# Pairs of w_in cut into scaled fp16 parts instead of fp32r parts

## The chip, the cores and the metric

One Trainium2 chip, one core of it. The metric is the device time of one execution in microseconds (us). The core has a matrix engine (TensorE, PE in the profile, with its weight loads as PEld), a vector engine (VectorE, DVE), a scalar engine (ScalarE, ACT), a general engine (GpSimd, POOL), and SyncE (SP), which here issues the transfers. Each engine works through its own queue in order and waits for the others by semaphores.

## The reference

One layer of a diffusion backbone, for 128 context tokens and 512 latent tokens (640 columns in all), width 1024. All inputs are fp32.

```
u = rms_norm(h, g_pre1) * (1 + sc1) + sh1
z = u @ w_in                      # 1024 x 6656: q, k, v, b_gate, c_gate, x_in, g_att, g_conv
q, k normalised per head, axial rotary on latent tokens
att  = block_attention(q, k, v) @ w_att_out
conv = (b_gate * dwconv3(c_gate * x_in)) @ w_conv_out
merged = sigmoid(g_att) * att + sigmoid(g_conv) * conv
h = h + g1 * rms_norm(merged @ w_o, g_post1)
u = rms_norm(h, g_pre2) * (1 + sc2) + sh2
h = h + g2 * rms_norm((silu(g) * val) @ w_down, g_post2)   # g, val = dwconv3(u @ w_up)
```

The shifts, scales and gates (sh1, sc1, g1, ...) come from a small product of two conditioning vectors with w_ada. The change concerns `u @ w_in` for the columns of g_att (all but the first 256), c_gate, x_in, b_gate and g_conv.

## The kernel before

**Precision.** A product of two fp32 matrices is made of three matmuls: each operand x is cut into hi, x rounded to fp32r (ScalarE, a copy), and lo = x - hi (VectorE), and hi*hi + hi*lo + lo*hi is summed in PSUM. The pools `whi` and `wlo` hold three such cuts of 128 x 1024 each.

**Stages.** Attention first; then eight products with w_att_out (`plain_gemm`, j = 0 to 7), in which the right operands of the next stage are made (`making`); then the stage of the 19 pairs; then eight products with w_conv_out, then w_o, and the feed-forward part, about half of the span.

**The pairs.** A pair is 256 columns of w_in (two raw tiles a1 and a2 of 128 x 1024, the reduction's eight blocks side by side). `PAIRS` lists them: GA 1 to 3, then four times C, X, B, then GC 0 to 3; pair 0 is the first. `mix` computes a pair with 640 tokens as a 2 x 2 block product by Strassen's method in Winograd's form: seven products instead of eight, each with 12 matmuls of 320 columns (four blocks of the reduction, three matmuls each). The seven, in the order of TensorE, are A11, A12, S2, S1, S3, S4, A22. Their left operands are four "parts" of weights: part 0 is a1 itself (A11, A12), part 1 holds two sums of the pair's blocks (S1, S2), part 2 two further sums (S3, S4), part 3 half of a2 (A22). The sums are made by VectorE (`msums`, three steps adds[0], adds[1], adds[2]), the cuts by `mhi` (ScalarE) and `lo_of` (VectorE). The right operands are the blocks B11, B21, B22 of u and four combinations T1 to T4 of them, all cut once for the stage; in the trace B blocks are read from UH and UL, the T from MT.

Between products ScalarE copies partial results out of PSUM (`copied`: p1 after A11, u2 after S2, p5 after S1; `mix_last` after A22) and VectorE adds them (`added`). S3 accumulates into the bank that u2 is copied from.

**Order.** In this part the queues of PE, ACT and DVE are the order of the code: `mix(m)` also issues the first cuts and sums of pair m + 1, and `extra` holds what follows from pair m - 1, by slots 0 to 6 between the products: after GA and GC two sigmoids, after GA two multiplications, after X the multiplications, two copies and taps of the convolution (L1564, L1565, L1500), after B the last tap, the multiplications and the cut of the finished rows (BHa, BHb by L1506, BL). SP's queue is put in order by a scheduler.

**Loads.** `mload` loads one raw tile (512 KB) into a pool of three, two per pair. `SHIFTS` says in which pair and slot a step of the second shift vector is made (`shift_add`: two instructions of 768 columns on VectorE, L342, then the load of the next row block into the one buffer XG). `shift_rows` and `shift_columns` fold the result with matmuls and transfers.

Of the kernel before, what the change touches and what calls it, by code (L numbers as in the profile page):

```python
# [112 lines left out]
def trunk_layer(ctx, tc, x_prompt, x_sample, cache_k, cache_v, c, c_ctx, w_ada, b_ada, g_pre1, g_post1, g_pre2,  # L113
# [1192 lines left out]
    for i in range(2):  # L1306
        for h in range(2):
            TT[f"mB{i + 1}{h + 1}"] = tuple(x[:, 4 * i:4 * i + 4, h * HT:(h + 1) * HT] for x in (UH, UL))
    TAG = {"T1": "r5a", "T2": "r5b", "T3": "r6a", "T4": "r6b"}
# [6 lines left out]
    def whole(out, name):  # L1316
        hi, lo = TT["m" + name]
# [8 lines left out]
    making = [  # L1326
        lambda: whole(Xa, "B11"), lambda: whole(Xb, "B12"), lambda: minus(Xa, Xa, Xb), lambda: whole(Xc, "B22"),
        lambda: right_of("T1", Xa), lambda: minus(Xb, Xc, Xb), lambda: minus_both(Xc, Xa, Xc), lambda: right_of("T3", Xb),
        lambda: whole(Xd, "B21"), lambda: right_of("T2", Xc), lambda: minus_both(Xd, Xc, Xd), lambda: right_of("T4", Xd)]
# [25 lines left out]
    def mload(n):  # L1355

        if n < 2 * NP:
            x, i = PAIRS[n // 2]
            col_load(("m", n // 2, n % 2), w_in, AT[x] + (2 * i + n % 2) * 128)
        elif n < 2 * NP + KT:  # L1360
            col_load(("v", n - 2 * NP), w_conv_out, (n - 2 * NP) * 128)
# [21 lines left out]
    def mix(m, extra):  # L1383
# [3 lines left out]
        pair["m", m] = tuple(bank((3 * m + i) % 8)[:, 0:HT] for i in range(3))  # L1387
# [12 lines left out]
        lo_of(("m", m, 1))  # L1400
# [9 lines left out]
        lo_of(("m", m, 2))  # L1410
# [6 lines left out]

        copied(("m", m), "p5", 2, HT)
# [6 lines left out]

        added(d1[:, HT:], ("m", m), "p5", 0)
        lo_of(("m", m, 3))
        mload(2 * m + 4)
        if nxt:
            mhi(nxt, 0)  # L1430
            lo_of(("m", nxt, 0))
            adds[1]()
        else:
            vcut(0)
# [8 lines left out]
        mload(2 * m + 5)  # L1443
# [6 lines left out]
    def times(out, a, b, sign=1.0):  # L1450
        if sign == 1.0:
# [9 lines left out]
    for j in range(KT):  # L1461
        unit = next_unit()
        if j == 6:
            for n in range(3):
                mload(n)
        if j < 6:
            for f in making[2 * j:2 * j + 2]:
                f()
        elif j == 7:
            adds = msums(0)  # L1470
            adds[0]()
            mhi(0, 0)
            lo_of(("m", 0, 0))
# [3 lines left out]
            mload(3)  # L1477
# [24 lines left out]
    def sigma(x, sign=1.0):  # L1502
        S.activation(x, x, AF.Sigmoid, scale=sign)
# [8 lines left out]
    XG = region(ra, "r2b", [5 * 512], F32, "XG")  # L1512
    xaccs, xraw = [[XG[:, i * 768:i * 768 + 768]] for i in range(2)], XG[:, 1536:2304]
    SHIFTS = {(0, 4): 0, (1, 1): 1, (2, 1): 2, (3, 1): 3, (4, 4): 4, (7, 4): 5, (10, 1): 6, (10, 4): 7}
# [26 lines left out]
    for m, (x, i) in enumerate(PAIRS):  # L1541
        ex = {}
        if m == 11:
            shr = shift_rows()
        elif m == 14:
            shift_columns(shr, bank(5))
# [6 lines left out]
        if before[0] in ("GA", "GC"):  # L1553
            r0, r1 = mrows(m - 1)
            also(1, sigma, r0)
            also(1, sigma, r1, -1.0)
# [12 lines left out]
        elif before[0] == "B":  # L1569
            c0, c1, y0, y1, b0, b1 = ROWS[:6]  # L1570
            also(0, conv_tap, y1, c1, o, 2)
            also(1, times, y0, b0, y0)
            also(1, b_hi, e, y0)
            also(1, times, y1, b1, y1, -1.0)
# [13 lines left out]
    sigma(ROWS[6])  # L1588
    sigma(ROWS[7], -1.0)
# [24 lines left out]
    for j in range(KT):  # L1614
# [4 lines left out]
        if 0 < j < KT - 3:  # L1619
            mload(2 * NP + j + 3)  # L1620
# [11 lines left out]
        outs = plain_gemm(j + 2, hi, lo, BH, BL)  # L1632
        sg = ROWS[j]
# [891 lines left out]
```

## Time and profile before

| | |
|---|---|
| median of 3 runs | 1074.8 us (1074.75 to 2641.38) |
| span of the profiled execution, first to last instruction | 1073.0 us |
| its mean granted TensorE clock | 0.999 |
| stage of the 19 pairs | 286.28 to 520.75 us of the span, 234.47 us |
| PE busy in that stage | 234.47 us |
| DVE busy in that stage | 196.91 us |
| ACT busy in that stage | 115.41 us |

The profiled execution is given with its span only; its own time lies above that by what comes ahead of the first and after the last instruction, which for the median is 1.8 us. One of the three runs, 2641.38 us, stands alone; the other two are 0.05 us apart.

In a row of the timeline the first number is the start in us from the span's start, the second the duration, then engine, line, instruction, output <- inputs, shapes (out <- in), count, and in brackets the idle time before it and what ended it. A row that stands for several instructions has the duration from the first start to the last end. Rows of groups give total busy time and the mean duration in ns; after the second bar the idle time of the engine ahead of them. TensorE's matmuls overlap, so the time of one in a stream is read from start to start.

### The profile page before, as it was taken

The page shows a single profiled execution, that of the slowest core. Times are in us where ns is not written, and L with a number is a line of the kernel's source. Part 1 is how long each engine was busy: PE and PEld are TensorE (multiplying, and loading weights), DVE is VectorE, ACT ScalarE, POOL GpSimd, SP SyncE. Part 2 cuts the span into 40 slices and gives each one's busy share as a digit, 9 for nine tenths or more (in the row PEclk, how much of TensorE's full clock was granted, in tenths as well). Part 3 has the DMA queues.
Part 4 walks back from the last instruction along what each step waited for, and adds up shares of the span by engine and source line. Part 5 has one row for each costly group of instructions (what it writes and reads, how often), then busy time and mean ns, then how long its engine had stood idle before and what let it go on. Part 6 is the DMA issues. An engine that isn't in the chain of part 4 may idle for free.

```text
span 1073.0 us, 20652 instructions
## 1 busy us (share of the span) xinstructions
PE 1056.8 (98%) x8216; PEld 995.4 (93%) x8216; DVE 899.9 (84%) x1379; ACT 598.4 (56%) x1057; POOL 133.1 (12%) x162
## 2 busy tenths in 40 slices
PE   8999999999999999999999999999999999999997
PEld 6788898899999999999998789999999999999996
DVE  5699999865498999896599678889999988989897
ACT  5478999942344544445322366645555555546673
POOL 1087676500000000000000020000000000000001
PEclk9999999999999999999999999999999999999999
DMA  9829999962244333223668634434544534436873
GB/s 320 256 82 175 190 168 187 191 147 60 75 123 124 93 103 94 79 79 99 189 188 253 198 131 129 121 116 136 166 131 152 150 122 131 152 116 219 277 275 115
DMA packets 243197, 164.02 MB, mean 153 GB/s; under 512 B 94874, under 2 KB 216214, under 8 KB 243102
## 3 DMA queue, kind: packets, MB, share of 16 engines
q1 hardware_dynamic: 242990, 162.68, 55.5%
q8 instruction: 64, 1.05, 0.4%
q14 instruction: 31, 0.25, 0.1%
q10 hardware_dynamic: 112, 0.04, 0.0%
HBM read 123.31 MB, written 17.36 MB: 131 GB/s over the span
## 4 chain that ended last, share of the span: by engine, by line
PE 90%; DVE 3%; ACT 2%; DMA 1%; POOL 1%; issue 1%; SPq 1%; DVEq 0%; ACTq 0%; POOLq 0%
PE b L1274 47%; PE b L235 10%; PE b L237 10%; PE b L236 9%; PE s L709 4%; PE s L1073 2%; PE s L1170 2%; PE s L235 1%; PE s L237 1%; PE s L1162 1%; PE s L478 1%; DVE marks L1120 1%; PE s L236 1%; PE b L1900 1%; ACT P L1134 1%
## 5 line engine op out<-in xcount | busy, mean ns | idle before, releaser
L1274 PE MATMUL b<-ZBr,whi 128*128 128x320 f32 x688 | 152.1, 309 | 0.0
L1274 PE MATMUL b<-MT,whi 128*128 128x320 f32 x608 | 134.4, 309 | 0.0
L1274 PEld LDWEIGHTS b<-ZBr,whi 128*128 128x128 f32 x688 | 114.9, 188 | 0.1
L1274 PE MATMUL b<-ZBr,wlo 128*128 128x320 f32 x344 | 106.1, 308 | 0.0
L1274 PEld LDWEIGHTS b<-MT,whi 128*128 128x128 f32 x608 | 101.7, 188 | 0.0
L1274 PE MATMUL b<-MT,wlo 128*128 128x320 f32 x304 | 94.0, 309 | 0.0
L1261 ACT ACTIVATE whi<-SUM 128x1024 fp32r<-128x1024 f32 x40 | 42.2, 1055 | 78.3 <-DVE SUM L1813 75.7
L1843 DVE SCALAR_TENSOR_TENSOR Y<-C,cffn,Y 128x642 f32<-128x642 f32 x88 | 77.9, 886 | 0.9
L1261 ACT ACTIVATE whi<-WB 128x1024 fp32r<-128x1024 f32 x38 | 40.2, 1058 | 55.5 <-DVE WB L1368 55.5
L1274 PE MATMUL b<-ZBT,whi 128*128 128x320 f32 x320 | 71.0, 308 | 0.0
L1274 PE MATMUL b<-UL,whi 128*128 128x320 f32 x228 | 70.8, 311 | 0.0
L1274 PE MATMUL b<-UH,wlo 128*128 128x320 f32 x228 | 70.1, 307 | 0.0
L1274 PE MATMUL b<-UH,whi 128*128 128x320 f32 x228 | 69.7, 306 | 0.0
L1282 ACT ACTIVATE p<-b 128x320 f32<-128x320 f32 x78 | 34.1, 437 | 55.3 <-PE b L1274 53.5
L1274 PEld LDWEIGHTS b<-ZBr,wlo 128*128 128x128 f32 x344 | 64.6, 188 | 0.0
L1265 DVE TENSOR_TENSOR wlo<-raw,whi 128x1024 fp32r<-128x1024 f32 (+1 forms) x51 | 50.4, 1020 | 13.4 <-ACT whi L1261 13.4
L1274 PEld LDWEIGHTS b<-MT,wlo 128*128 128x128 f32 x304 | 57.1, 188 | 0.0
L1274 PEld LDWEIGHTS b<-ZBT,whi 128*128 128x128 f32 x320 | 54.2, 188 | 1.6
L1120 DVE TENSOR_REDUCE marks<-s 128x1 f32<-128x640 f32 x64 | 52.1, 817 | 4.0 <-PE s L1073 3.8
L1265 DVE TENSOR_TENSOR wlo<-WB,whi 128x1024 fp32r<-128x1024 f32 x38 | 46.5, 1224 | 8.8 <-ACT whi L1261 8.7
L2355 POOL TENSOR_TENSOR ssqs<-ssqs 128x1 f32<-128x1 f32 x4 | 1.4, 356 | 412.9 <-ACT GJ L2349 412.9
L1261 ACT ACTIVATE whi<-raw 128x1024 fp32r<-128x1024 f32 (+1 forms) x51 | 43.5, 892 | 15.4 <-DMA raw<-in_w_o_dram 12.5
(477 smaller groups left out, 3348.1 us busy)
## 6 DMA issues: line engine op xcount, KB each, us to landing
raw<-in_w_in_dram SPq DMA_DIRECT2D x48, 512.0 KB
RAW<-in_w_up_dram SPq DMA_DIRECT2D x40, 512.0 KB
raw<-in_w_down_dram SPq DMA_DIRECT2D x22, 512.0 KB
GA<-in_w_ada_dram SPq DMA_DIRECT2D x16, 512.0 KB
actd<-Y SPq DMA_DIRECT2D x18, 321.0 KB
actl<-ACTb SPq DMA_DIRECT2D x18, 321.0 KB
A<-actl SPq DMA_DIRECT2D x9, 642.0 KB
A<-actd SPq DMA_DIRECT2D x9, 642.0 KB
```

What stands on the lines that cost most here:

```text
L235: PE.matmul(out, ah, bh, start=start, stop=False)
L236: PE.matmul(out, ah, bl, start=False, stop=False)
L237: PE.matmul(out, al, bh, start=False, stop=stop)
L709: PE.matmul(out, a, b, start=start and n == 0, stop=stop and n == 2, skip_group_check=True)
L1073: PE.matmul(o[h], q_of(hl, i, rows), kk[kx][rows, g, ks], start=m == 0, stop=m == 2, tile_position=(64 * h, 0), skip_group_check=True)
L1120: V.tensor_reduce(out=mk[:, h:h + 1], in_=s_of(), axis=AX.X, op=ALU.max, negate=True)
L1170: PE.matmul(p[64 * h:64 * h + 64, i * 128:i * 128 + 128], VH[:, w, s, vc_], src, start=k == 0 and m == 0, stop=k == ks[-1][0] and m == 2, ...
L1261: S.activation(to[0], raw, AF.Copy)
L1265: V.tensor_tensor(out=lo, in0=raw, in1=hi.bitcast(F32), op=ALU.subtract)
L1274: PE.matmul(out, p[:, ws], q[:, k, :], start=start and k == 0 and n == 0, stop=stop and k == 3 and n == 2, skip_group_check=True)
L1282: S.activation(t, pair[j][b], AF.Copy)
L1843: V.scalar_tensor_tensor(out=y, in0=crows(j)[i][:, d:d + NACT], scalar=cffn[:, 44 * d + o:44 * d + o + 1], in1=y, op0=ALU.mult, op1=ALU.add)
```

## The change

The pairs' operands are cut into fp16 parts instead of fp32r parts, each multiplied by a scale that the kernel finds from sums of squares.

- **Right operands.** All seven (B11, B21, B22, T1 to T4) are now cut anew into fp16 hi and lo, times C1, two operands to a tile. C1 comes from a bound: ScalarE sums squares of the modulation vectors, `total_of` adds them over partitions with a fp32 matmul that has a broadcast column as weights and two columns of ones, and `scale_of` makes an approximate inverse square root by arithmetic on the float's bits (VectorE, one column).
- **Left operands.** Per pair, ScalarE squares both raw tiles in one instruction of 2048 columns with an accumulated sum (`msquare`, L1397), `total_of` (L1319) sums over partitions, `scale_of` (L1323) gives the scale, and GpSimd makes the factors that undo it (`mscale`). `mhi` (L1433) is a copy with that scale, `mlo` (L1437) a multiplication and subtraction in one instruction. The factor is undone in the sigmoids and in the multiplications after B.
- **Raw weights.** Three pairs are kept in the regions r0 and r1, which UH and UL leave; a pair is loaded after part 3 of the pair three before it. The first three are issued at j = 4 instead of one by one from j = 6. The pool of three raw tiles holds only columns of w_att_out and w_conv_out.
- **Shift vector.** XG moves to the end of r1; five of its eight steps move from the pairs 3 to 10 to the pairs 15 to 17, its fold from pairs 11 and 14 to pair 18 and the second product with w_conv_out.

The number of matmuls with 320 columns stays the same. The core of the diff:

```diff
-    TAG = {"T1": "r5a", "T2": "r5b", "T3": "r6a", "T4": "r6b"}
+    SHARED = {"r5a": ("T1", "T2"), "r5b": ("T3", "T4"), "r6a": ("B11", "B21"), "r6b": ("B22",)}
+    def total_of(p, sums):
+        for i, a in enumerate(sums):
+            PE.matmul(p[:, 400:402], a.broadcast_to((128, 128)), ones[:, 0:2], start=i == 0, stop=i == len(sums) - 1, skip_group_check=True)
+    def scale_of(out, p):
+        V.tensor_scalar(out=out.bitcast(I32), in0=p[:, 400:401].bitcast(I32), scalar1=-0.5, scalar2=MAGIC, op0=ALU.mult, op1=ALU.add)
...
-        z = rb.tile([128, 2, 4, HT], F32R, tag=TAG[name], name=f"M{name}")
+            fp16s[tag] = rb.tile([128, 2, 2, 4 * HT], F16, tag=tag, name=f"M{tag}")
...
-        S.activation(hi, x, AF.Copy)
-        V.tensor_tensor(out=lo, in0=x, in1=hi.bitcast(F32), op=ALU.subtract)
+        S.activation(hi, x, AF.Copy, scale=C1)
+        V.scalar_tensor_tensor(out=lo, in0=x, scalar=C1, in1=hi, op0=ALU.mult, op1=ALU.subtract)
...
+    def msquare(m):
+        junk = fp16s["r6b"][:, 1].rearrange("p i c -> p (i c)").bitcast(BF16)[:, 0:2048]
+        S.activation(junk, both_raw(m).rearrange("p i c -> p (i c)"), AF.Square, accum_out=SSQ)
+    def mscale(m, p):
+        scale_of(dscale(m), p)
+        x = PAIRS[m][0]
+        G.tensor_scalar(out=unscale(m), in0=dscale(m), scalar1=C1, scalar2=None, op0=ALU.mult)
+        G.tensor_tensor(out=unscale(m), in0=unscale(m), in1=MINUS, op=ALU.pow)
...
-        hi_of(("m", m, part), src)
+        to = tuple(wp.tile([128, 1024], F16, tag=x, name=nm(x), bufs=3)[:, :n] for x in ("whi", "wlo"))
+        S.activation(to[0], src, AF.Copy, scale=dscale(m))
+    def mlo(m, part):
+        raw, hi, lo = cut["m", m, part]
+        V.scalar_tensor_tensor(out=lo, in0=raw, scalar=dscale(m), in1=hi, op0=ALU.mult, op1=ALU.subtract)
...
-        lo_of(("m", m, 2))
+        mlo(m, 2)
+        if nxt:
+            msquare(nxt)
         more(2)
         step("S2")
...
         step("S1")
+        if nxt:
+            total_of(full[1], [SSQ])
         copied(("m", m), "p5", 2, HT)
...
         step("S3")
+        if nxt:
+            mscale(nxt, full[1])
         added(d1[:, HT:], ("m", m), "p5", 0)
-        lo_of(("m", m, 3))
-        mload(2 * m + 4)
+        mlo(m, 3)
+        if m + 3 < NP:
+            mload(m + 3)
...
-    def sigma(x, sign=1.0):
-        S.activation(x, x, AF.Sigmoid, scale=sign)
+    def sigma(x, m, sign=1):
+        S.activation(x, x, AF.Sigmoid, scale=unscale(m, sign))
...
-    SHIFTS = {(0, 4): 0, (1, 1): 1, (2, 1): 2, (3, 1): 3, (4, 4): 4, (7, 4): 5, (10, 1): 6, (10, 4): 7}
+    SHIFTS = {(0, 4): 0, (1, 1): 1, (2, 1): 2, (15, 4): 3, (16, 1): 4, (16, 4): 5, (17, 1): 6, (17, 4): 7}
```

ScalarE's queue in a pair that follows a B pair, from the copy p1 on, before (BHa are the two finished rows, whi the hi part of part 2 and then of part 3):

```order
L1282 ACTIVATE p1_272_5123<-b2_269_5104 128x320
L1506 ACTIVATE BHa_5126<-WA_3814 128x640
L1261 ACTIVATE whi_273_5141<-WB_3815 128x1024
L1506 ACTIVATE BHa_5126<-WA_3814 128x640
L1282 ACTIVATE u2_275_5160<-b2_269_5104 128x320
L1282 ACTIVATE p5_276_5175<-b4_271_5106 128x320
L1261 ACTIVATE whi_277_5177<-raw_252_4959 128x512
```

The same place in the changed kernel (RAWM holds the raw pairs, scal the scales; L1397 is the square of the next pair):

```order
L1282 ACTIVATE p1_258_5160<-b2_255_5141 128x320
L1589 ACTIVATE BHa_5163<-WA_3814 128x640
L1433 ACTIVATE whi_259_5178<-WB_3815,scal_3816 128x1024
L1397 ACTIVATE Mr6b_4107,scal_3816<-RAWM0_4113 128x2048
L1589 ACTIVATE BHa_5163<-WA_3814 128x640
L1282 ACTIVATE u2_261_5198<-b2_255_5141 128x320
L1282 ACTIVATE p5_262_5214<-b4_257_5143 128x320
L1433 ACTIVATE whi_263_5216<-RAWM0_4113,scal_3816 128x512
```

The square is new and stands ahead of the second BHa and of the copies u2 and p5.

TensorE in the same pair of the changed kernel, from the last matmul of S1 to the first of S3 (before, the two products follow each other, and no weight load is an instruction of its own):

```order
L1274 LDWEIGHTS wlo_254_5125
L1274 MATMUL b4_257_5143<-Mr5a_3979,wlo_254_5125 128x320
L1319 MATMUL b3_256_5142<-ones_88,scal_3816 128x2
L1274 LDWEIGHTS whi_259_5178
L1274 MATMUL b2_255_5141<-Mr5b_4046,whi_259_5178 128x320
```

The total of the squares stands between the two products, and the loads of fp16 weights are instructions.

VectorE in pair 17 (the third of GC), from the addition of p1 on, before:

```order
L1285 TENSOR_TENSOR WB_3815<-b4_448_6525,p1_450_6541 128x320
L1265 TENSOR_TENSOR wlo_452_6558<-WB_3815,whi_451_6557 128x1024
L1368 TENSOR_TENSOR WB_3815<-raw_446_6510 128x512
L1368 TENSOR_TENSOR WB_3815<-raw_441_6486,raw_446_6510 128x512
L1285 TENSOR_TENSOR WB_3815<-b3_447_6524,p5_454_6588 128x320
L1265 TENSOR_TENSOR wlo_456_6591<-raw_430_6387,whi_455_6590 128x512
```

and the same pair in the changed kernel, from what now stands ahead of that addition:

```order
L342 SCALAR_TENSOR_TENSOR RAWM1_4114<-RAWM1_4114,s32_83 128x768 x2
L1285 TENSOR_TENSOR WB_3815<-b4_410_6591,p1_412_6607 128x320
L1437 SCALAR_TENSOR_TENSOR wlo_414_6627<-WB_3815,scal_3816,whi_413_6626 128x1024
L1421 TENSOR_TENSOR WB_3815<-RAWM0_4113 128x512 x2
L342 SCALAR_TENSOR_TENSOR RAWM1_4114<-RAWM1_4114,s32_83 128x768 x2
L1323 TENSOR_SCALAR scal_3816<-b4_410_6591 128x1
L1285 TENSOR_TENSOR WB_3815<-b3_409_6590,p5_416_6659 128x320
L1437 SCALAR_TENSOR_TENSOR wlo_418_6662<-RAWM1_4114,scal_3816,whi_417_6661 128x512
```

Two shift steps have come in, one ahead of the addition of p1 and one ahead of the scale (L1323) and of the lo part of part 3.

More of the change, by code (lines that the diff above doesn't have):

```diff
@@ L1386, in mix @@
         nxt = m + 1 if m + 1 < NP else None
-        pair["m", m] = tuple(bank((3 * m + i) % 8)[:, 0:HT] for i in range(3))
+        full = [bank((3 * m + i) % 8) for i in range(3)]
+        pair["m", m] = tuple(x[:, 0:HT] for x in full)
         def step(x):
@@ L1542, in trunk_layer @@
         ex = {}
[L1543 removed]
+        if m == NP - 1:
             shr = shift_rows()
[L1545 to L1546 removed]
         def also(slot, f, *args):
@@ L1571, in trunk_layer @@
             also(0, conv_tap, y1, c1, o, 2)
-            also(1, times, y0, b0, y0)
+            also(1, times, y0, b0, y0, unscale(m - 1))
             also(1, b_hi, e, y0)
-            also(1, times, y1, b1, y1, -1.0)
+            also(1, times, y1, b1, y1, unscale(m - 1, -1))
             also(2, b_hi, o, y1)
@@ L1632, in trunk_layer @@
         outs = plain_gemm(j + 2, hi, lo, BH, BL)
+        if j == 1:
+            shift_columns(shr, bank(2))
         sg = ROWS[j]
```

98 lines of the change are left out of this document (71 added, 27 removed).

## The prediction, made before the changed kernel was run

> **What bounds the kernel now.** I read the page first, then TensorE's windows over the stage that the change touches, then the timeline of single matmuls in it, then the groups of VectorE and ScalarE by shape.
>
> ```profile
> span 1073.0 us, 20652 instructions
> PE 1056.8 (98%) x8216; PEld 995.4 (93%) x8216; DVE 899.9 (84%) x1379; ACT 598.4 (56%) x1057; POOL 133.1 (12%) x162
> 286.28:520.75 234.47, 234.47 (x1607) 233.43 (x1606) 196.91 (x283) 115.41 (x180) 0.00 (x0) 1.00 0.33 96
> ```
>
> The third line is the stage of the 19 pairs (columns: stretch, length, then busy time of PE, PEld, DVE, ACT, POOL, granted clock, DMA share, GB/s): TensorE is busy through all of its 234.47 us at full clock, VectorE for 84%, ScalarE for 49%. So a cheaper matmul shows in the time, until something else makes TensorE wait. One pair has seven products of 12 matmuls. Two pairs in the timeline, from the first product of one to the first product of the next but one:
>
> ```profile
> 384.45 0.31 PE L1274 MATMUL b<-UH,whi 128*128 128x320 f32 x1
> ...
> 408.99 0.31 PE L1274 MATMUL b<-UH,whi 128*128 128x320 f32 x1
> ```
>
> 24.54 us for 168 matmuls: 146 ns each, 12.26 us a pair (12.27, within reading). 19 x 12.26 = 232.9; the rest of 234.47 is mostly the folding of the shift rows. No weight load or copy is late here.
>
> **What the matmuls become.** 19 x 84 = 1596 matmuls of 320 columns go from fp32r to fp16. The trace has no fp16 matmul of 320 columns. The nearest rows are 256 columns in both widths, and 128 columns in fp16:
>
> ```profile
> 161.81 0.28 PE L709 MATMUL s<-whi,UH 128*128 128x256 f32 x1
> ...
> 162.52 0.28 PE L709 MATMUL s<-whi,UH 128*128 128x256 f32 x1
> 63.55 0.82 PE L947 MATMUL s<-P,some 128*128 128x256 bf16 x6
> L947 PE MATMUL s<-P,some x6: 272/272/273, 63.6 to 64.1; 128*128 128x256 bf16 x6
> 155.33 1.01 PE L1170 MATMUL s<-PT,VV 128*64 128x128 f16 x30
> 156.17 0.39 PE L1162 MATMUL s<-ident,marks 128*64 128x128 f32 x4
> ```
>
> fp32r: six steps in 0.71 us, 118 ns. 16 bits: (820 - 272) / 5 = 109.6 ns. fp16 at 128 columns: 15 side-by-side pairs in 0.84 us, 56 ns. The 16-bit line rises (109.6 - 56) / 128 = 0.42 ns a column, so 320 columns take 109.6 + 64 x 0.42 = about 136 ns; I take 135.7. Bounds: 146 (no gain) and 133. A product falls from 1.75 to 1.63 us, a pair's 84 from 12.26 to 11.40, the stage by 19 x 0.86 = 16.3 us. The order shows a separate weight load before each fp16 matmul; the six bf16 matmuls have theirs too and keep 109.6 ns, so I cost that at nothing; uncovered it would be the 109.6's own margin, under 10 ns each.
>
> Against this the Trainium skill, page "TensorE: Matmul & The Clock Gate", section "Back-to-back issue gap", gives a stream of loads and matmuls about 81 ns at 128 columns and 131 ns at 512. By that, 320 columns would take an estimated 106 ns (estimate from that page). The trace disagrees at both widths it has: 56 and 109.6 ns. It is a rival below.
>
> **What is added on TensorE.** One `total_of` per scale, a fp32 matmul with two columns (18 in the stage, 3 ahead of it). The nearest row is the fold with 32 columns, one instruction in two records:
>
> ```profile
> 250.80 0.30 PE L319 MATMUL b<-sel,WB 128*128 128x32 f32 x2
> 250.93 0.39 PE L235 MATMUL b<-AHa,whi 128*128 128x320 f32 x1
> 251.16 0.31 PE L236 MATMUL b<-AL,whi 128*128 128x320 f32 x1
> ```
>
> 0.36 us less one ordinary step of 0.146: 0.22 us. Where it must wait for its input I add 0.16 us, since its weights can only be loaded then (a load of this shape overlaps the step before it otherwise): 0.38. If nothing waited, the stage would win 16.3 - 18 x 0.22 = 12.3 us. It waits, and ScalarE's queue says where.
>
> **ScalarE's queue.** The rows of the order in the section on the change show it: after a B pair the square of the next pair's raw weights (L1397, 2048 columns) stands between the hi part of part 2 and the second BHa, ahead of the copies u2 and p5; in every other pair it stands between that hi part and u2. On TensorE the matmul L1319 waits for the square, between the fourth product S1 and the fifth, S3; S3, S4, A22 and all that follows is queued behind it. S3 also overwrites the bank that u2 copies, so it waits for u2. Prices:
>
> ```profile
> L435 ACT ACTIVATE junk<-XT x5: 1057/1057/1059, 4.7 to 10.8; 128x1024 f32<-128x1024 f32 x5
> L435 ACT ACTIVATION_READ_ACCUMULATOR junk<-XT x5: 186/186/189, 5.6 to 11.8; 128x1 f32 x5
> L1261 ACT ACTIVATE whi<-raw 128x512 fp32r<-128x512 f32 x19 | 11.9, 625 | 0.0
> L1261 ACT ACTIVATE whi<-WB 128x1024 fp32r<-128x1024 f32 x38 | 40.2, 1058 | 55.5 <-DVE WB L1368 55.5
> L1564 ACT ACTIVATE WA<-WA,feat 128x640 f32<-128x640 f32 x4 | 3.3, 828 | 0.9 <-DVE WA L1452 0.8
> L1506 ACT ACTIVATE BHa<-WA 128x640 fp32r<-128x640 f32 x4 | 2.9, 733 | 2.9 <-DVE WA L1452 2.9
> L1500 DVE SCALAR_TENSOR_TENSOR WA<-WA,feat 128x511 f32<-128x511 f32 x16 | 12.0, 748 | 0.0
> L1368 DVE TENSOR_TENSOR WB<-WB,raw 128x512 f32<-128x512 f32 x38 | 26.1, 686 | 0.0
> ```
>
> From 512 to 1024 columns an ACTIVATE grows by 433 ns, so 2048 take 1.058 + 0.866 = 1.92 us, with the accumulator's read (0.19, starting 0.09 early) 2.02. A scale that is a column instead of a constant costs 828 - 733 = 95 ns on ScalarE and 748 - 686 = 62 ns on VectorE; every cut of the pairs now has one (bounds 0 and these): hi parts 1.15 us, lo parts 1.28.
>
> Now the timeline of the pair after a B pair, whose first product starts at 396.71 (408.99 less a pair), and the whi of the pair after an X pair (start 384.45):
>
> ```profile
> 388.72 1.05 ACT L1261 ACTIVATE whi<-WB 128x1024 fp32r<-128x1024 f32 x1
> 400.58 0.74 ACT L1506 ACTIVATE BHa<-WA 128x640 fp32r<-128x640 f32 x1 [1.47 <-DVE WA L1452]
> 401.23 1.05 ACT L1261 ACTIVATE whi<-WB 128x1024 fp32r<-128x1024 f32 x1
> 402.18 0.73 ACT L1506 ACTIVATE BHa<-WA 128x640 fp32r<-128x640 f32 x1
> 402.81 0.42 ACT L1282 ACTIVATE u<-b 128x320 f32<-128x320 f32 x1
> ```
>
> After X the whi starts 4.27 us into the pair, after B 4.52. Both hang on VectorE's queue, which doesn't get shorter: behind the fifth product it still does the same work, while the two products that cover it lose 0.25 us, and two lo parts gain 0.06 each. So both start 0.37 later in the new pair: 4.64 and 4.89. (On one engine the next instruction starts 0.09 us before the last ends.)
>
> After X: whi ends 5.79, square 5.70 to 7.72. Four products end at 4 x 1.63 = 6.51. L1319 starts at 7.76, a wait of 1.25. The pair: 11.40 + 1.25 + 0.38 = 13.03.
> After B: square 5.95 to 7.97, wait 1.5; 0.38; then the second BHa and u2 run to about 8.97, S3 waits another 0.6. The pair: 11.40 + 1.5 + 0.38 + 0.6 = 13.88.
> After a gate pair GA or GC: copy p from 1.83, two sigmoids with a scale column (828 ns, 0.73 apart), whi from 3.63, square 4.7 to 6.7: wait 0.24, pair 12.02.
> After C, and the first: the square ends near 5.3, no wait: 11.62.
>
> **The moved shift adds.** Five of the eight move from the pairs 3 to 10 to the pairs 15 to 17 (of 0 to 18). By the order they stand on VectorE ahead of the scale and of the lo part that A22 needs. Their rows load into one buffer, so the second add of a pair waits for a transfer started by the first:
>
> ```profile
> 411.30 1.94 DVE L342 SCALAR_TENSOR_TENSOR XG<-XG,s 128x768 f32<-128x768 f32 x2
> ...
> 416.62 1.02 DVE L342 SCALAR_TENSOR_TENSOR XG<-XG,s 128x768 f32<-128x768 f32 x1 [0.33 <-DMA XG<-in_w_ada_dram]
> ```
>
> From the end of one, 413.24, to the next, 416.62, are 3.4 us. In pairs 16 and 17 the first adds end at 4.7, the second run 8.15 to 10.05, lo ends near 11.2 where A22 could start at 10.4: wait 0.85, pair 12.02 + 0.87 = 12.89. In pair 15 (after a B pair) one shift add, two instructions with 1.86 us of VectorE, goes before the lo part, which had 0.4 us to spare: A22 waits 1.45, 13.88 + 1.45 = 15.33.
>
> **The sum.** 5 x 11.62 + 3 x 12.02 + 4 x 13.03 + 3 x 13.88 + 15.33 + 2 x 12.89 + 11.40 (the last, without a scale) = 240.4 against 232.9: +7.5. Three totals ahead: +0.7. The three more cuts of right operands run on ScalarE and VectorE beside six products of 7 us, the earlier loads of six 512 KB columns beside the same; I cost them at nothing (if a w_att_out column came late behind them, up to 3 us). GpSimd's four small operations per scale are used a pair later: nothing. 1073.0 + 8.2 = 1081.2, and with the 1.8 us between this span and the median of 1074.8: **1083**.
>
> **The rivals.** (1) The waits hide: columns as scales cost nothing, and the copies come in time. Speaking for it: ScalarE is idle half of the stage. Against: its queue is in order. 12.3 - 0.7 gained, 1.7 of it lost to the transfers: 1065. 0.12. (2) fp16 keeps 146 ns. For: nothing measured at 320. Against: 109.6 and 118. The 16.3 us stay, but S1 ends 0.5 us later and the queue's 0.25 isn't lost: 0.75 less wait in each of the eight pairs after X and B, 0.24 in three after GA, some 0.9 in the three with shift adds. 7.5 + 16.3 - 6 - 0.7 - 2.7 = +14.4, with the 0.7 ahead: 1090. 0.1. (3) By the page's rate, as a mechanism: matmuls of 106 ns end S1 at 5.1, but squares still end at 7.7 and 8.0, and behind them VectorE's lo parts are late. Pairs without a wait get 10.0 (VectorE again), after GA 11.8, after X 12.7, after B 13.9, the three with shift adds as above, the last 10.4: 50 + 35.4 + 50.8 + 41.7 + 41.1 + 10.4 = 229.4, 3.5 under 232.9: 1072. 0.04; both rows speak against it. (4) Slower by over 2%: the square itself, at its place between S1 and S3. Each microsecond more goes into the 11 pairs that wait for it (3 after GA, 4 after X, 4 after B), 11 us in all; from 3.3 us on (1.6 times my 2.02) the sum passes 1096. For: a bf16 output and an accumulator over 2048 columns stand in no row. Against: 1057 ns for 1024. 1098. 0.12.
>
> **How the numbers follow.** The forecast has 0.6; its own range is 1076 to 1091 (scale columns free 1077, both waits 0.3 us longer 1090). Left over, 0.02, is a gain above 2%, which 133 ns with every wait hidden doesn't reach. For eight in ten I go from 1066 to 1093. Within 2%, about what can be told from no change: 1053.3 to 1096.3. Faster 0.02, same 0.86, slower 0.12.
>
> **What would show it.** In the trace after: L1274 in fp16 at about 136 ns a step; L1397 near 2.0 us; TensorE waits at L1319 <- ACT of 1.2 to 1.5 us after X and B pairs and none after C; a wait for L342 and lo in pairs 15 to 17. Wrong, if TensorE shows no such waits, if the step is at 146, or if a wait stands at the start of the products instead.

## The result and the profile after

The changed kernel takes 1085.36 us (median of four runs, 1084.29 to 1086.47), the kernel before on the same chip 1075.48 us: a ratio of 1.0095 (95% interval 1.0079 to 1.011), no change by the 2% bound and 10 us slower in fact. The one run of the kernel before at 2641.38 us is in its median and not in the ratio. The forecast was 1083.

The span from the page of the changed kernel, and the window of the 19 pairs (columns as in the prediction):

```profile
span 1084.3 us, 20865 instructions
286.89:531.40 244.51, 229.17 (x1642) 160.84 (x1641) 204.12 (x300) 155.59 (x216) 23.86 (x54) 0.99 0.30 86
```

The stage took 234.47 us before and takes 244.51 now; ahead of it stand 0.6 us more, behind it 0.65 (552.25 to 552.9). So 10 of the 11.3 us by which the span grew lie in the stage. TensorE, busy all of it before, now idles for 15 us in it. The three largest of its waits in the same stretch (line waited at, releaser and its line: us in all, times, longest):

```profile
PE b L1319 <- ACT Mr6b L1397: 10.6, 10, 1.3
PE b L1274 <- ACT u L1282: 2.2, 4, 0.6
PE b L351 <- DVE WB L1285: 0.9, 1, 0.9
```

The wait for the square at the total is the largest. In pairs 15 to 17 the last product waits, as forecast, for what stands behind the shift adds in VectorE's queue: in pair 15 0.65 us for the addition of p5 and 0.23 for the lo part. Single pairs show more. In order these are pair 4 (after C), 5 (after X), 6 (after B), 9 (after B) and 17:

```profile
334.12:345.67 11.55, 11.55 (x89) 8.39 (x87) 8.33 (x14) 7.25 (x10) 1.25 (x4) 1.00 0.32 91
345.67:358.73 13.06, 11.88 (x88) 8.43 (x86) 12.42 (x21) 8.81 (x12) 0.86 (x2) 1.00 0.28 81
358.73:374.25 15.52, 13.63 (x88) 9.13 (x86) 13.22 (x20) 9.75 (x13) 1.53 (x3) 0.89 0.32 92
398.87:412.72 13.85, 11.95 (x89) 8.43 (x87) 12.27 (x19) 8.61 (x12) 1.08 (x3) 1.00 0.27 76
505.36:520.10 14.74, 13.18 (x97) 8.41 (x94) 13.50 (x20) 9.70 (x13) 2.34 (x4) 1.00 0.10 29
```

Pairs 6 and 9 do the same work and wait for the same things, yet pair 6 is 1.67 us longer, and its mean granted clock is 0.89 (the third column from the end). Pair 12 is again 15.52 us at 0.89. The timeline of TensorE in pair 6, and ScalarE's rows at that place:

```profile
365.12 0.30 PE L1274 MATMUL b<-Mr5a,wlo 128*128 128x320 f16 x1
366.75 0.38 PE L1319 MATMUL b<-ones,scal 128*128 128x2 f32 x2 [1.33 <-ACT Mr6b L1397]
367.69 0.43 PE L1274 MATMUL b<-Mr5b,whi 128*128 128x320 f16 x2 [0.56 <-ACT u L1282]
...
368.50 0.43 PE L1274 MATMUL b<-Mr5b,whi 128*128 128x320 f16 x2
368.77 0.36 PE L1274 MATMUL b<-Mr5b,wlo 128*128 128x320 f16 x1
368.93 0.74 PE L1274 MATMUL b<-Mr5b,whi 128*128 128x320 f16 x2
369.46 0.47 PE L1274 MATMUL b<-Mr5b,wlo 128*128 128x320 f16 x1
```

```profile
364.71 1.89 ACT L1397 ACTIVATE Mr6b<-RAWM 128x2048 bf16<-128x2048 f32 x1
366.51 0.19 ACT L1397 ACTIVATION_READ_ACCUMULATOR Mr6b<-RAWM 128x1 f32 x1
366.60 0.72 ACT L1589 ACTIVATE BHa<-WA 128x640 fp32r<-128x640 f32 x1
367.23 0.41 ACT L1282 ACTIVATE u<-b 128x320 f32<-128x320 f32 x1
```

This is the predicted queue, one row behind the other: the square, the second BHa, u2; TensorE waits for the first and for the last. But from 368.9 on two matmuls take 0.53 us from start to start (368.93 to 369.46) where they had taken 0.27 (368.50 to 368.77): half clock, until 372.3. That was not in the prediction. In pair 17 the surprise is at the fold of the shift rows, which stands behind the pair's last product:

```profile
519.31 0.85 PE L351 MATMUL b<-RAWM,ones 128*32 128x384 f32 x8 [0.91 <-DVE WB L1285]
```

It writes the PSUM bank (number 5) that holds pair 17's product S4, which VectorE has still to add to u2. Where the fold stood before, pair 10 used the banks 6, 7 and 0.

### The profile page after: what moved, and what is told of

Read it like the earlier page. It is cut to its first block, busy times and chain, and to the rows that moved or that the text cites. A ratio compares the mean times of both kernels' runs of the same rounds, so it can differ in the third digit from the quotient of the medians.

```text
span 1084.3 us, 20865 instructions
## 1 busy us (share of the span) xinstructions
PE 1053.6 (97%) x8258; PEld 924.2 (85%) x8258; DVE 912.6 (84%) x1402; ACT 645.5 (60%) x1102; POOL 158.6 (15%) x220
## 4 chain that ended last, share of the span: by engine, by line
PE 77%; DVE 10%; ACT 7%; DMA 3%; issue 2%; POOL 0%; SPq 0%; DVEq 0%; ACTq 0%
PE b L1274 36%; PE b L235 10%; PE b L237 9%; PE b L236 9%; PE s L709 3%; DVE wlo L1437 2%; ACT whi L1433 2%; PE s L1073 2%; PE s L1170 2%; ACT Mr6b L1397 1%; DVE marks L1120 1%; DMA PT<-P 1%; DVE WB L1421 1%; PE s L235 1%; DMA XT<-in_w_ada_dram 1%
## 5 line engine op out<-in xcount | busy, mean ns | idle before, releaser
L1274 PEld LDWEIGHTS <-whi 128*128 128x128 f16 x1064 | 105.9, 100 | 44.8 <-issue 4.6
L1274 PEld LDWEIGHTS <-wlo 128*128 128x128 f16 x532 | 52.4, 99 | 22.5 <-DVE wlo L1437 1.7
L1433 ACT ACTIVATE whi<-WB,scal 128x1024 f16<-128x1024 f32 x38 | 43.4, 1143 | 43.5 <-DVE WB L1421 43.5
L1274 PE MATMUL b<-Mr5b,whi 128*128 128x320 f16 x304 | 63.7, 301 | 3.1 <-ACT u L1282 2.2
L1274 PE MATMUL b<-Mr6a,whi 128*128 128x320 f16 x304 | 62.5, 299 | 0.0
L1274 PE MATMUL b<-Mr5a,whi 128*128 128x320 f16 x304 | 62.5, 299 | 0.0
L1437 DVE SCALAR_TENSOR_TENSOR wlo<-WB,scal,whi 128x1024 f16<-128x1024 f32 x38 | 48.7, 1282 | 10.0 <-ACT whi L1433 10.0
L1274 PE MATMUL b<-ZBT,wlo 128*128 128x320 f32 x160 | 49.4, 309 | 0.0
L1265 DVE TENSOR_TENSOR wlo<-SUM,whi 128x1024 fp32r<-128x1024 f32 x40 | 48.7, 1216 | 0.0
L709 PE MATMUL s<-whi,UH 128*128 128x256 f32 x160 | 47.9, 299 | 0.1
L1274 PE MATMUL b<-Mr5b,wlo 128*128 128x320 f16 x152 | 46.0, 303 | 0.7 <-DVE wlo L1437 0.7
```

Of the source, the lines that this page charges most:

```text
L709: PE.matmul(out, a, b, start=start and n == 0, stop=stop and n == 2, skip_group_check=True)
L1265: V.tensor_tensor(out=lo, in0=raw, in1=hi.bitcast(F32), op=ALU.subtract)
L1274: PE.matmul(out, p[:, ws], q[:, k, :], start=start and k == 0 and n == 0, stop=stop and k == 3 and n == 2, skip_group_check=True)
L1433: S.activation(to[0], src, AF.Copy, scale=dscale(m))
L1437: V.scalar_tensor_tensor(out=lo, in0=raw, scalar=dscale(m), in1=hi, op0=ALU.mult, op1=ALU.subtract)
```

## The experiments

The theory: TensorE waits for the square because of its place in ScalarE's queue; the half clock follows from the idle time; and under both, VectorE's queue is what keeps the cheaper matmuls from showing. The rivals stand with each run. Ratios are to the kernel before in the same rounds.

**The square a pair earlier**, ahead of the hi part of part 1; that of pair 1 ahead of the stage.

```diff
-        if nxt:
-            msquare(nxt)
...
             mhi(nxt, 0)
+            if m + 2 < NP:
+                msquare(m + 2)
             mlo(nxt, 0)
```

> The square of a pair's raw weights is taken one pair earlier, in ScalarE's idle time before the hi part of part 1. My theory: the 10.6 us that TensorE waits at the total (L1319) behind the square go, and with them the two stretches of half clock (about 1.7 us each). What is left in the pairs after X and after B is VectorE's own work, 12.4 and 13.2 us busy in the changed kernel, so these stay at 12.5 and 13.2; the others fall to 11.6 and 11.75; pairs 15 to 17 keep their shift adds. By the prediction's recurrence the stage loses 5.3 us, with the clock 8.7: about 1077 against 1085.4. Rival 1: the half clock has nothing to do with the waits: about 1080. Rival 2: the square only marks where VectorE is late, and its wait moves to the lo parts: no more than 2 us gained, 1083 or above.

1077.89 us, ratio 1.0026 (1.0017 to 1.0036): 7.5 us less than the changed kernel, where 8.7 were expected; between the two profiled executions the stage alone lost 8.7. The windows of the stage and of the pairs 5 and 6, and the three largest of TensorE's waits in the stage:

```profile
287.48:523.27 235.79, 224.43 (x1642) 157.95 (x1641) 203.55 (x300) 154.49 (x214) 32.10 (x54) 1.00 0.31 89
345.31:357.69 12.38, 11.86 (x88) 8.19 (x86) 11.76 (x20) 8.33 (x11) 1.30 (x2) 1.00 0.27 79
357.69:370.96 13.27, 12.11 (x88) 8.38 (x86) 12.10 (x19) 8.43 (x13) 2.22 (x3) 1.00 0.27 79
```

```profile
PE b L1274 <- ACT u L1282: 3.7, 4, 0.9
PE b L1274 <- DVE wlo L1437: 3.5, 10, 0.5
PE b L1274 <- DVE WA L1285: 2.6, 2, 1.8
```

The total is in none of the rows of that view any more, and no stretch at half clock is left in this profile. The pairs after GA fell to 11.6, those after X and B to the lengths expected of VectorE's side (12.5 and 13.2). ScalarE does as much as before; only the place changed.

**The shift adds in early pairs.**

```diff
-    SHIFTS = {(0, 4): 0, (1, 1): 1, (2, 1): 2, (15, 4): 3, (16, 1): 4, (16, 4): 5, (17, 1): 6, (17, 4): 7}
+    SHIFTS = {(0, 4): 0, (1, 1): 1, (2, 1): 2, (3, 1): 3, (4, 4): 4, (7, 4): 5, (10, 4): 6, (13, 4): 7}
```

> The five shift adds that the change put into pairs 15 to 17 go back to early pairs (3, 4, 7, 10, 13, where VectorE is busy for 7 to 10 of 11.6 us). My theory: pair 15 falls from 15.06 to 13.85, pair 16 from 12.84 to 11.89, pair 17 from 14.74 to about 12.75 (the fold of the shift rows stays at its end, without its 0.9 us of waiting): 4.1 us less, 1081.3; the pairs 3, 4, 7, 10, 13 stay as they are. Rival: the adds cost VectorE the same wherever they stand and only move the lateness: no change, 1085.4.

1081.35 us, ratio 1.0064 (1.0045 to 1.0083). The pairs 15, 16 and 17 (the last with the fold):

```profile
475.83:489.68 13.85, 11.96 (x88) 8.42 (x86) 12.27 (x19) 8.61 (x12) 1.07 (x3) 1.00 0.26 77
489.68:501.57 11.89, 11.89 (x89) 8.42 (x86) 8.36 (x14) 8.57 (x12) 1.05 (x3) 1.00 0.12 33
501.57:514.66 13.09, 12.84 (x97) 8.49 (x94) 9.24 (x14) 9.69 (x13) 1.05 (x3) 1.00 0.00 1
```

3.8 us less in the three (42.64 to 38.83 us), and the early pairs kept their lengths within 0.02 us: VectorE had time there. Of the fold's 0.9 us of waiting 0.3 remain, so the bank it shares with pair 17 costs that much even where VectorE is not late.

**No squares.** The total is taken of a column set once (FIXED); the sum of squares is left out.

```diff
+    FIXED = scal[:, 94:95]
+    G.memset(FIXED, 2.0)
...
-            msquare(nxt)
...
-            total_of(full[1], [SSQ])
+            total_of(full[1], [FIXED])
```

> Leaves out the squares: the total is taken of a fixed column instead of the sum of squares of the pair's weights (the total, the scale and the columns stay). My theory: the same stage as with the square taken a pair ahead, within 1 us, about 1077, since ScalarE has the time for it where nothing is queued behind it. Rival: the square costs by being there at all (ScalarE's copies behind it): over 1.5 us less than the kernel that takes it ahead.

1078.28 us, ratio 1.003 (1.002 to 1.004), the same as with the square taken a pair ahead. So 2 us of ScalarE a pair cost nothing where nothing waits behind them, and the rival falls.

**No squares, totals or scales made of them.** What is left of the change is the fp16 parts, cut with a column as scale, and the shift adds and the fold at their new places; the finding of the scale is left out.

```diff
+    G.memset(scal[:, 0:24], 1024.0)
...
-        scale_of(dscale(m), p)
...
-            msquare(nxt)
...
-            total_of(full[1], [SSQ])
```

> Leaves out the squares, the totals and the scales that are made of them: the scale columns are set once to 1024. What is left of the change is the fp16 parts with a column as scale. My theory: where a pair is bound by TensorE the total's 0.22 us goes (11.63 to 11.41), where it is bound by VectorE nothing does: 1.1 us less in the stage than with the fixed sum, and 0.5 of the total ahead of the stage: about 1075. Rival: TensorE is the bound in all pairs, and all 18 totals count, 4.0 us and 0.5: about 1072.

1074.19 us, ratio 0.9992 (0.9982 to 1.0002). Even with the whole price of the scale gone nothing is won against the kernel before: the pairs 5 and 6 still take 12.38 and 12.89 us, with VectorE busy for 11.92 and 11.95 of them, and pair 15, with a shift add and a stretch at half clock, 15.42. The 0.8 us below the expected figure is no more than the runs spread.

**Matmuls in the wait.** 24 matmuls that nobody reads, ahead of the total in the pairs after B.

```diff
+            if m and PAIRS[m - 1][0] == "B":
+                w, x = TT["mB11"][0][:, 0, 0:128], TT["mB11"][0][:, 1, 0:104]
+                for n in range(24):
+                    PE.matmul(full[1][:, 404:508], w, x, start=True, stop=True, skip_group_check=True)
             total_of(full[1], [SSQ])
```

> The changed kernel with 24 extra matmuls of 104 columns, on operands long at hand and into columns nobody reads, ahead of the total in the four pairs after a B pair: at 56 ns each (the 128-column fp16 rate) they take 1.3 of the 1.5 us that TensorE waits there, so they cost nothing by themselves. My theory: the half clock comes from TensorE's idle time in those pairs (1.5 and 0.7 us close together, when both fall into one stretch of the clock's own counting), so it goes: all 19 pairs at 136 ns a step, pairs 6 and 12 at 13.85 us, about 1082.5, with no run near 1086. Rival: the clock falls at times of its own, whatever TensorE waits for: two drops stay in the profile, 1085.4 and runs that lie 1.7 us apart as before.

1084.64 us, ratio 1.0081 (1.0066 to 1.0096). In its profile no pair ran at half clock and the stage took 241.28 us, 3.2 less than in the changed kernel. The median had moved by 0.7 us only, with intervals that overlap, so both kernels were run again side by side in five rounds.

> The changed kernel unchanged, on the same chip and in the same rounds as the one with the 24 extra matmuls. My theory: its idle time in the pairs after B (1.3 and 0.7 us within 2.8 us) puts TensorE at half clock for 3.4 us where both fall into one of the clock's stretches of 3.41 us, so the profile shows one to three drops among the pairs 6, 9, 12 and 15, not the same ones in every run, and the runs spread by multiples of 1.7 us: median 1085.4. Rival: the drops belong to fixed places: again pairs 6 and 12, and no spread.

> The 24 extra matmuls again, beside the changed kernel itself, since the first median (1084.64) did not show the 3.3 us that its profiled stage had won. My theory: no drop in any pair of the stage, which is 241.3 us long again; the median lies below that of the changed kernel beside it by 1.7 us a drop that it had, some 2 to 3 us. Rival: drops at times of their own are seen here too, and the medians agree within 0.5 us.

The changed kernel took 1086.09 us (ratio 1.0102, 1.0086 to 1.0118), the one with the extra matmuls 1083.47 (1.0082, 1.0069 to 1.0095): 2.6 us apart, in the direction expected, though the intervals overlap. The windows say more. First the changed kernel, run again (pairs 6, 9 and 15; 12 is like 6), then the one with the extra matmuls (pairs 9 and 15; 6 and 12 are like 9):

```profile
359.40:373.25 13.85, 11.95 (x89) 8.43 (x87) 12.27 (x19) 8.61 (x12) 1.08 (x3) 1.00 0.27 77
397.86:413.38 15.52, 13.62 (x88) 9.12 (x86) 13.38 (x21) 9.76 (x13) 1.39 (x3) 0.89 0.32 92
...
476.46:491.99 15.53, 13.63 (x89) 9.10 (x86) 13.87 (x20) 8.61 (x12) 2.35 (x3) 0.89 0.31 87
```

```profile
398.06:411.91 13.85, 13.05 (x113) 9.63 (x111) 12.27 (x19) 8.61 (x12) 1.08 (x3) 1.00 0.27 77
...
474.98:490.04 15.06, 13.38 (x112) 9.55 (x110) 13.39 (x19) 8.61 (x12) 2.22 (x3) 1.00 0.30 87
```

The same program drops its clock in pairs 6 and 12 in one execution and in 9 and 15 in another; with TensorE kept busy it drops in none of eight such pairs in two executions, and the pairs keep their 13.85 us although each does 24 matmuls more (pair 15 its 15.06). The timeline there has the extra matmuls in the place of most of the wait:

```profile
366.11 1.26 PE L1485 MATMUL b<-Mr6a 128*128 128x104 f16 x24
367.61 0.38 PE L1319 MATMUL b<-ones,scal 128*128 128x2 f32 x2 [0.23 <-ACT Mr6b L1397]
```

So the rival that drops have times of their own falls.

**The square ahead and the shift adds early, together.** Both diffs above.

> The square a pair ahead and the shift adds in early pairs, together. My theory: the two gains have little in common (the square acts in the pairs after GA, X and B, the shift adds in the last three): stage 230.7 us by the recurrence and 0.9 for the fold, 231.6 against 235.8 with the square alone; about 1073.5, 1.3 us less than the kernel before. VectorE is the bound in the pairs after X (12.4) and after B (13.2). Rival: what the shift adds cost VectorE appears again in the early pairs once TensorE no longer waits there: 1077.

1074.38 us, ratio 0.9986 (0.9977 to 0.9995); the stage takes 231.14 us. The gains, 7.5 and 4.0 us alone, are 11.0 together; the rival shows in one pair only, pair 3 with a shift add in it (11.55 us with the square alone, 11.89 here). Beside the fold's 0.3 us two waits are left, and both hang on VectorE's queue (u2 stands behind BHa, which waits for VectorE's product):

```profile
PE b L1274 <- ACT u L1282: 3.7, 4, 0.9
PE b L1274 <- DVE wlo L1437: 3.2, 9, 0.5
```

**Half of the weight sums on GpSimd.** As the last kernel, and the first two sums of each pair made by GpSimd (E):

```diff
-        def both():
-            add(s1, a2[:, 0:512], a2[:, 512:1024])
-            add(s3, a1[:, 0:512], a2[:, 0:512])
+        def both(E=V):
+            E.tensor_tensor(out=s1, in0=a2[:, 0:512], in1=a2[:, 512:1024], op=ALU.add)
+            E.tensor_tensor(out=s3, in0=a1[:, 0:512], in1=a2[:, 0:512], op=ALU.add)
```

> As the kernel with both, and the two first sums of each pair's raw weights (2 x 512 columns, 0.68 us each on VectorE, 36 of the 72 sums in all) are made by GpSimd. My theory: VectorE's work is what holds the pairs after X and B, so 1.2 us less of it a pair shortens the pairs after B from 13.2 to 12.2 (those after X are held by an earlier step and stay at 12.4); GpSimd takes 1.4 us for each and has the time: stage 226.4 and 0.9, about 1069, faster than the kernel before by 6 us. Rival: GpSimd's two-operand adds slow VectorE's own instructions beside them (lo parts above 1.28 us), or their sums come late: no gain, 1073.5 or more.

1085.11 us, ratio 1.0089 (1.0072 to 1.0106): 10.7 us slower than without it. The rival holds. First one place in this kernel, two shift adds of VectorE and between their starts a sum of GpSimd; then all 14 shift adds of the stage (shortest, median and longest in ns) and the additions with one tensor in PSUM:

```profile
301.88 1.01 DVE L342 SCALAR_TENSOR_TENSOR RAWM<-RAWM,s 128x768 f32<-128x768 f32 x1
302.04 1.98 POOL L1424 TENSOR_TENSOR WB<-RAWM 128x512 f32<-128x512 f32 x1 [5.47 <-DVE wlo L1437]
302.80 2.03 DVE L342 SCALAR_TENSOR_TENSOR RAWM<-RAWM,s 128x768 f32<-128x768 f32 x1
...
L342 DVE SCALAR_TENSOR_TENSOR RAWM<-RAWM,s x14: 1006/1519/2037, 301.9 to 461.6; 128x768 f32<-128x768 f32 x14
...
L1285 DVE TENSOR_TENSOR WA<-b,p 128x320 f32<-128x320 f32 x24 | 11.6, 484 | 11.9 <-PE b L1274 11.7
```

The same two groups in the kernel that it was made from:

```profile
L342 DVE SCALAR_TENSOR_TENSOR RAWM<-RAWM,s x14: 1010/1014/1018, 302.3 to 453.8; 128x768 f32<-128x768 f32 x14
...
L1285 DVE TENSOR_TENSOR WA<-b,p 128x320 f32<-128x320 f32 x24 | 11.7, 488 | 8.7 <-PE b L1274 8.7
```

The two shift adds do equal work. The first is running when the sum starts and takes its 1.01 us; the second starts beside the sum and takes 1.0 us more. Of the 14, seven take 1.01 to 1.02 us and seven 2.02 to 2.04 (the median lies between and is the time of none); of the taps with 511 columns eight take 0.74 and eight 1.76. In all, 27 instructions of VectorE that start beside a sum take 1.0 to 1.1 us more, and three lo parts 0.4 to 0.5. Those that read one of two tensors from PSUM (the last rows: b is a PSUM bank) keep their time. VectorE's busy time in the stage rose from 203.22 to 210.99 us, although 36 sums of 0.69 us had left it, and the stage from 231.14 to 243.09; about 3.4 us of that are two stretches at half clock.

**The work beside the products, later.** As the kernel with both, nothing added or left out; only the slots of the work that follows from X and B are others (slot 2 lies behind hi and lo of part 2, slot 5 behind the cuts of the next pair's part 0).

```diff
-            also(1, lambda: S.activation(y0, c0, AF.Copy, scale=taps_of(e)[1]))
...
-            also(1, conv_tap, y0, c0, e, 0)
...
-            also(3, conv_tap, y1, c1, o, 0)
+            also(2, lambda: S.activation(y0, c0, AF.Copy, scale=taps_of(e)[1]))
...
+            also(2, conv_tap, y0, c0, e, 0)
...
+            also(5, conv_tap, y1, c1, o, 0)
...
-            also(1, b_hi, e, y0)
-            also(1, times, y1, b1, y1, unscale(m - 1, -1))
-            also(2, b_hi, o, y1)
-            also(2, b_lo, e, y0)
-            also(3, b_lo, o, y1)
+            also(2, times, y1, b1, y1, unscale(m - 1, -1))
+            also(2, b_hi, e, y0)
+            also(4, b_hi, o, y1)
+        if m > 1 and PAIRS[m - 2][0] == "B":
+            i = PAIRS[m - 2][1]
+            also(1, b_lo, 2 * i, ROWS[2])
+            also(1, b_lo, 2 * i + 1, ROWS[3])
```

> As the kernel with the square ahead and early shift adds, and the work beside the products is put behind what TensorE waits for: after an X pair ScalarE's y0 and y1 and VectorE's taps stand behind hi and lo of part 2 (the last tap behind the next pair's lo), after a B pair the second product, the first BHa and the second stand behind them as well, and the two BL rows go into the pair after, where VectorE idles for 3 us. Nothing is added or left out. My theory: in the pairs after X (12.4 us) and B (13.3) TensorE waits for part 2 only because it is queued behind this work on engines that wait for each other; with 12.4 and 13.2 us of work in two pairs and 7.3 in the third, VectorE has the time. All pairs 11.6 to 11.9: stage 221.8 by the recurrence and 0.9, 222.7 against 231.1; about 1066, faster than the kernel before by 9 us. Rival: VectorE's amount of work bounds these pairs, 12.4 and 13.2 us busy: no more than 1 us gained, 1073.5.

1064.86 us (1064.31 to 1065.82), ratio **0.9908** (0.9892 to 0.9925): faster than both kernels, by 9.7 us than the one before in the same rounds. The stage, the pairs 5 (after X) and 6 (after B), and the largest wait that is left in the stage:

```profile
287.80:511.05 223.25, 221.88 (x1643) 158.34 (x1641) 201.70 (x300) 155.58 (x214) 35.54 (x54) 1.00 0.32 94
345.96:357.50 11.54, 11.54 (x88) 8.39 (x86) 11.08 (x18) 8.77 (x11) 1.30 (x2) 1.00 0.35 99
357.50:369.05 11.55, 11.55 (x88) 8.36 (x86) 11.33 (x19) 8.68 (x13) 2.35 (x3) 1.00 0.30 89
```

```profile
PE b L1274 <- DVE wlo L1437: 0.8, 4, 0.2
```

The pairs 5 and 6 took 26.9 us at full clock in the changed kernel (13.06 and, as pair 9, 13.85); 25.7 with the square ahead and early shift adds, now 23.1. Against that last kernel the stage is 7.9 us shorter (231.14 to 223.25) while VectorE's work in it is nearly the same (203.22 us busy, 201.70 now), so its amount was not the bound: its order was.

**The kernel before, with the same reordering.** The last diff alone, with the constant signs of the kernel before.

> The kernel before with the same reordering of the work beside the products alone (fp32r parts as they were). My theory: TensorE is busy through the whole stage at 146 ns a step, so nothing is gained: 1074.8, within 1 us; what the reordered fp16 kernel gains is then the fp16 step's. Rival: the reordering itself is what gains: 1070 or below.

1076.07 us, ratio 1.0013 (1.0003 to 1.0022): no gain, and 0.5 us more than the theory allowed. The stage takes 0.9 us more than before (235.41 us); in pair 10, which has two shift adds, the last product now waits 0.51 us for VectorE's addition of p5, a wait that the kernel before has not. The reordering alone gains nothing while TensorE takes 146 ns a step; it pays because fp16 made TensorE's part shorter.

**Fixed scales, with the side work later.** The diffs of the fixed scale, the early shift adds and the later side work.

> Leaves out the squares, the totals and the scales made of them (columns set once to 1024), with early shift adds and the side work later. My theory: with VectorE out of the way TensorE is the bound, and each of the 18 totals in the stage counts its 0.22 us: 4.0, and 0.5 ahead, 4.5 less than the same kernel with squares a pair ahead, about 1061.5. Rival: VectorE is still as late as TensorE in the pairs after X and B, and the totals hide behind it: 1.5 less, 1064.5.

1060.66 us, ratio 0.987 (0.9856 to 0.9885), 4.2 us less than with the scales that the kernel finds. By the time the theory holds; by the windows only half of it does. An early pair (1) here and in the kernel with its scales:

```profile
298.07:309.48 11.41, 11.41 (x86) 8.22 (x84) 11.11 (x15) 6.90 (x10) 0.00 (x0) 1.00 0.44 123
```

```profile
299.36:310.91 11.55, 11.55 (x89) 8.39 (x87) 11.09 (x16) 8.58 (x11) 2.29 (x3) 1.00 0.44 123
```

A total costs 0.14 us where nothing waits, 2.5 for 18, not 4.0. Most of the rest of the stage's 4.8 us came from pairs 8 to 15, which are 11.7 to 11.9 us long in the kernel with its scales and 11.4 to 11.5 here. In pair 8 there, TensorE waits 0.21 us for a lo part, ahead of which VectorE's queue has the scale's column (L1323).

## Why the prediction was right, and where its terms were off

- **The fp16 step** was forecast at 135.7 ns. Pair 1 without a total (fixed scales, side work later) takes 11.41 us for 84: 135.8. The bounds 133 and 146 were not needed, and the weight loads, costed at nothing, show no cost. The 16.3 us are there: in that kernel, where only the fold still waits (0.3 us), the stage takes 218.42 us, 16.05 less than in the kernel before. The rivals with 146 ns (1090) and with 106 (1072) are out. By the Trainium skill's page "TensorE: Matmul & The Clock Gate", section "Back-to-back issue gap", the step would be an estimated 106 ns; the trace differs, with 135.8.
- **The square** was forecast at 2.02 us; from its start to the end of its accumulator's read it is 1.99 (364.71 to 366.70), so the rival of 3.3 us and more (1098) is out. The pairs that wait for it were thirteen and not the eleven of that rival: 16 and 17 wait too, 0.33 and 0.26 us. The cuts with a column:

```profile
L1433 ACT ACTIVATE whi<-WB,scal 128x1024 f16<-128x1024 f32 x37 | 42.3, 1142 | 41.5 <-DVE WB L1421 41.5
L1437 DVE SCALAR_TENSOR_TENSOR wlo<-WB,scal,whi 128x1024 f16<-128x1024 f32 x37 | 47.4, 1281 | 9.5 <-ACT whi L1433 9.5
```

  1.15 and 1.28 us were forecast for the cuts.
- **The waits**, pair by pair: after GA 12.02 forecast, 11.89 measured; after X 13.03 and 13.06; after B 13.88 and 13.85 (without the half clock); with no wait 11.62 and 11.55; pair 15 15.33 and 15.06; pair 16 12.89 and 12.84; pair 17 12.89 and 13.05, without the fold (0.78) and its wait (0.91); the last 11.40 and 11.31. The rival that the waits hide (1065) is out for this kernel. Its reason, that ScalarE is idle half of the stage, came true only when the square was moved, and its time, 1065, only when VectorE's order was changed too.
- **Mis-sized: the total**, 0.22 us forecast, 0.14 measured; over the pairs this and small margins made the sum about 0.9 us too long. Taken from a fold with 32 columns, it had been priced by its nearest row and not by its size. Another 0.8 us too much stood in the 1.57 for the rest of the stage: the fold's own work took 0.78 there, and the transposition of the shift columns had gone behind the stage.
- **Missing: the half clock.** The step said of TensorE's waits only what they cost by themselves. In the profiled execution they brought 3.3 us on top (2 x 1.67), in other executions other amounts.
- **Missing: the bank of the fold.** It was left where it was in the sum; at its new place it waits 0.9 us for pair 17's last add.
- **Stage and span.** 240.4 for the pairs and 1.57 for the rest of the stage made 242.0 forecast, 244.5 measured: +3.3 and +0.9 for what was missing, -1.7 for what was too long. The 0.7 us ahead of the stage can't be told: in the profiles of the changed kernel and the experiments the stage starts anywhere from 286.3 to 288.7 us, earliest in the one with the fixed sum, which has the three totals ahead. The 0.65 us behind the stage was not forecast. Part of it is that transposition, which stood at 459.16 among the pairs and stands at 545.71 now, in the second product; the rest is open.

The mechanism was right, wait by wait. That the time was right to 0.2% was luck in part: 4.2 us were left out, and 1.7 of them were covered by terms priced too high.

## What to carry to other kernels

Making the busiest engine's instructions cheaper shows only as far as the other engines' queues let it: here 16 us of cheaper matmuls became 10 us of loss, and moving one instruction, which stood in a queue ahead of a copy and a total that TensorE needs, brought 7.5 back. When TensorE is sped up, go through each engine's queue and put behind every operand that TensorE waits for whatever has a later due time, into the next stretch if that has room; with that, the same change is worth 0.9%. Where TensorE's waits come to 1.5 to 2 us within some 3 us, price them up to 1.7 us higher, since the clock may halve behind them.

## What the runs showed of the hardware

**The clock falls behind about half a stretch of idling.** By the trace's record of the granted clock every drop in the stage lasts 3.41 us, and in one execution all changes of the clock lie whole multiples of 3.413 us apart: in the changed kernel the drops are 368.88 to 372.29 and 447.38 to 450.80, and the ends are 78.51 us or 23 x 3.413 apart. So an execution can be cut into such stretches from one change on. The stages of all profiles have nine drops: two in each of the changed kernel's two and in that with GpSimd's sums, one each with early shift adds, fixed sum and fixed scale. In the stretch ahead of it TensorE is idle (3.41 less its busy time) for 1.70 to 2.07 us in seven cases, and for 1.48 in the two with GpSimd's sums. The limit is not sharp by this measure: two stretches with 1.53 us with GpSimd's sums have no drop behind them, nor has one with 1.84 in the kernel with the square a pair ahead. A stretch of the changed kernel and the one behind it, then that other one with the one behind it:

```profile
365.47:368.88 3.41, 1.57 (x11) 1.19 (x12) 2.91 (x5) 3.10 (x6) 0.00 (x0) 1.00 0.00 0
368.88:372.29 3.41, 3.41 (x15) 1.98 (x13) 2.81 (x5) 1.15 (x1) 1.53 (x3) 0.50 0.02 6
```

```profile
479.29:482.70 3.41, 1.57 (x12) 0.88 (x9) 3.41 (x7) 0.65 (x1) 0.56 (x2) 1.00 0.00 0
482.70:486.11 3.41, 3.18 (x25) 2.20 (x24) 3.19 (x5) 3.27 (x4) 1.79 (x2) 1.00 0.81 212
```

TensorE is busy for 1.57 us in both, and only the first is followed by half clock; what tells them apart is not shown. The idle time need not be in one piece: in pair 6 it was 1.33 and 0.56 us by the waits. Which pair is hit depends on how the stretches fall on it, hence 6 and 12 once and 9 and 15 another time. The Trainium skill's page "TensorE: Matmul & The Clock Gate" has the free-running stretch of about 3.4 us (section "What's actually happening"), which the trace bears out with 3.413. Its advice to avoid idle gaps above some 3 us (section "Why this matters for your kernels") is too lenient here: gaps of 1.33 and 0.56 us in one stretch were enough.

**GpSimd's two-tensor adds hold up VectorE's.** An instruction of VectorE with two tensors in SBUF that started while a sum of GpSimd ran took 1.0 us more, whatever its own length: shift adds 2.03 us for 1.01, taps 1.76 for 0.74. One that was running already kept its time. One with a single tensor (L340) was held as well, 1.63 us for 0.61. The Trainium skill's "GPSIMD Engine Reference", section "Key points", says that the two share SBUF interfaces and contend where VectorE runs in a 2-port mode or has two SBUF inputs. The trace agrees for two inputs, and gives the price, 1.0 us for each instruction held.
